# Third weight sum of the odd gate-and-up blocks: from an accumulating transfer to an addition on VectorE

## The chip, the cores and the metric

The kernel runs on one core of one Trainium2 chip. The metric is the device time of one execution in microseconds (us); the median over several runs is compared. Engines are called PE (TensorE), DVE (VectorE), ACT (ScalarE), POOL (GpSimd) and SP (SyncE, which here only issues transfers).

## The reference, cut to what matters

One decoder layer on 512 tokens of width 1024: normalisation, an input projection, two mixers, an output projection, and then the part that the change touches, a dense feed-forward layer:

```
h = h + (silu(xn @ w_gate) * (xn @ w_up)) @ w_down      # xn = rms_norm(h), 512 x 1024
```

w_gate and w_up are 1024 x 2816 float32, w_down is 2816 x 1024. Everything is float32 and is computed as three matmuls over high and low parts.

## The kernel before, in words

**Blocks.** The hidden width of 2816 is cut into 11 blocks of 256 columns, q = 0 to 10. In each block gate and up are made together with a Strassen-like scheme of seven products in place of eight. Its seven weight operands come from four quarters of 512 x 256: gate rows 0 to 511 (b11), gate rows 512 to 1023 (b21), up rows 0 to 511, and up rows 512 to 1023 (b22). The operands are B11 = b11, B21 = b21, T1 = gate(0) + up(0), T2 = T1 + b22, T3 = up(0) + b22, B22 = b22, T4 = T2 + b21.

**Order of the products on PE.** `first_products(q)` runs B11 and B21, `last_products(q)` runs T2, T1, T3, B22, T4. One product is 24 matmuls of 128 x 128 against 256 columns; its result is added up by DVE (L1241 to L1267).

**Operands.** `put` turns each sum into a high part (ACT, L149) and a low part (DVE, L151, a subtraction 128 x 1024). High and low lie together in one of four buffers, two with the name whi and two with the name wlo, taken in turn.

**Loads.** `Weights(q)` loads b11 and b21 (L1145, L1146), `load_rest` loads gate(0) into t1 (L1173), b22 (L1174) and up(0) into t3 (L1175), each 512 KB and all issued by SP. Two accumulating transfers issued by POOL then add up(0) to t1 (L1177) and up(1) to t3 (L1178), in every block but q = 1. The block q = 1 loads up(0) once and makes T1 (L1183) and T3 (L1191) on DVE. `middle` makes t2 = t1 + b22 on DVE (L1184), `end` makes T3, B22 and T4 (L1194 adds b21 to t2).

**Buffers.** In even blocks t1, t2 and t3 are three buffers named t; in odd blocks they are slices of one buffer named L, and one such buffer serves all odd blocks in turn. b11 and b21 share one of three buffers named wraw, and b22 takes another. A load waits until the last reader of the buffer before it is done: L1173 of an odd block for the T4 low part of the odd block before it, L1174 for L1194 of the block before it.

**What sets the order.** The order on each engine is made at build time by a scheduler; instructions marked high priority go ahead as soon as it thinks them ready. The engines then run their own lists strictly in that order. On DVE, the sum L1184 of a block stands well ahead of that block's products: L1184 of an odd block q + 1 stands in front of L1241 and of the B22 low part of the even block q.

The functions that the change touches, and what calls them:

Of the kernel before, what the change touches and what calls it, by code (L numbers as in the profile page):

```python
# [13 lines left out]
OP = mybir.AluOpType  # L14
# [32 lines left out]
def hybrid_layer(ctx: ExitStack, tc: tile.TileContext, x, positions, norm_mix, w_in, mu_shift, w0, w2, a0, a2,  # L47
# [3 lines left out]
    PE, DVE, ACT, POOL = nc.tensor, nc.vector, nc.scalar, nc.gpsimd  # L51
# [16 lines left out]
    def st(shape, tag, bufs=1, dtype=F32):  # L68
        return sb.tile(list(shape), dtype, name=tag, tag=tag, bufs=SB_BUFS.get(tag, bufs))
# [3 lines left out]
    w_in, w_out, w_gate, w_up, w_down = (w.rearrange("l a b -> (l a) b") for w in (w_in, w_out, w_gate, w_up, w_down))  # L73
# [1062 lines left out]
    class Weights:  # L1136
# [25 lines left out]
        def load_rest(self):  # L1162
            self.b22 = st([128, 2048], "wraw")[:, 0:1024].rearrange("p (k n) -> p k n", n=256)
            if self.q % 2:
                tt = st([128, 4, HK, 256], "L")
                self.t1, self.t2, self.t3 = (tt[:, i] for i in range(3))
            else:
                self.t1, self.t2, self.t3 = (st([128, HK, 256], "t4") for _ in range(3))
            if self.q == 1:
                nc.sync.dma_start(self.t3, self.quarter(w_up, 0))  # L1170
                nc.sync.dma_start(self.b22, self.quarter(w_up, 1))
                return
            nc.sync.dma_start(self.t1, self.quarter(w_gate, 0))  # L1173
            nc.sync.dma_start(self.b22, self.quarter(w_up, 1))  # L1174
            nc.sync.dma_start(self.t3, self.quarter(w_up, 0))  # L1175
            with tc.high_priority():
                POOL.dma_start(self.t1, self.quarter(w_up, 0), accum_op=OP.add)  # L1177
                POOL.dma_start(self.t3, self.quarter(w_up, 1), accum_op=OP.add)  # L1178

        def middle(self, tag=None):  # L1180
            with tc.high_priority():
# [5 lines left out]

        def end(self):
            with tc.high_priority():
                if self.q == 1:  # L1190
                    DVE.tensor_add(self.t3, self.t3, self.b22)  # L1191
                self.put("T3", self.t3)
                self.put("B22", self.b22)
                DVE.tensor_add(self.t2, self.t2, self.b21)  # L1194
                self.put("T4", self.t2)
# [135 lines left out]
    for n, (a, b) in enumerate(GROUPS):  # L1331
        one, two = halves[n]
        a11, a21, a12, a22 = (h[:, :, x] for h in (one, two) for x in (left, right))
        lead, end = n == 0, n == 1
        t1, t2 = block4(a, 0, "wraw"), block4(b, 1, ("gin", "kB")[n])
        t3 = st([128, 4, 512], "wraw") if lead else None
        t3 = [t3[:, 2 * i:2 * i + 2] if lead else st([128, 2, 512], "t4") for i in range(2)]
        for i in range(2):
            nc.sync.dma_start(t3[i], down(a, 1)[:, 2 * i:2 * i + 2])
        t2s.append(t2)  # L1340
        DVE.tensor_sub(a21, a22, a21)
        multiply(m1, a_side(a11), b_side(t1), lead, end)
        DVE.tensor_add(a11, a21, a11)
        with tc.high_priority():
            for i in range(2):
                h = slice(2 * i, 2 * i + 2)
                DVE.tensor_add(t1[:, h], t1[:, h], t3[i])
                POOL.dma_start(t3[i], down(b, 1)[:, h], accum_op=OP.add)
            DVE.tensor_add(t2, t2, t1)
        multiply(m5, a_side(a21), b_side(t1), lead, end)  # L1350
        multiply(m6, a_side(a11), b_side(t2), lead, end)
        DVE.tensor_sub(a21, a11, a22)
        multiply(m7, a_side(a21), b_side(t3), lead, end)
# [81 lines left out]
```

## Time and profile before

| | |
|---|---|
| median of 3 runs | 745.86 us (743.71 to 747.25) |
| the profiled execution's own time | 746.93 us |
| its span, first to last instruction | 745.2 us |
| PE busy | 720.3 us, 97% |
| DVE busy | 591.9 us, 79% |
| ACT busy | 402.0 us, 54% |
| POOL busy | 150.8 us, 20% |
| transfers issued by POOL (queue q0) | 12.58 MB, 10.9% of the 16 transfer engines' span |
| transfers issued by SP (queue q1) | 71.91 MB, 29.4% |

The gate-and-up blocks lie between about 415 and 625 us of the span. A busy PE is not a PE at its peak, since its matmuls overlap and their ends are modelled; a product's length is read from the starts of its first matmul and of the next product's. Times in the rows are microseconds from the span's start.

### The profile page before, as it was taken

To read this page: it belongs to the slowest core of one execution; us is meant where nothing else is said; L and a number is where in the kernel's file an instruction comes from. 1 tells how busy PE (TensorE), PEld (TensorE's weight loads), DVE (VectorE), ACT (ScalarE), POOL (GpSimd) and SP (SyncE) were. 2 spreads that over 40 slices of the span, in tenths; PEclk is the share of its full clock that TensorE was granted. 3 is DMA by queue.
4 is the path that set the end of the run, shared out by engine and by line. 5 is a ranking of instruction groups with operands and counts; after the bars stand their busy time and mean duration, and the time that the engine had idled before them with its cause. 6 is when DMAs were issued, how large, how long until landed. Compare 5 with 4: busy or idle time off the path is not lost.

```text
span 745.2 us, 14931 instructions
## 1 busy us (share of the span) xinstructions
PE 720.3 (97%) x6045; PEld 627.3 (84%) x6045; DVE 591.9 (79%) x1097; ACT 402.0 (54%) x670; POOL 150.8 (20%) x250
## 2 busy tenths in 40 slices
PE   6999999998989999999999999989999999999996
PEld 6967887898878788777788999989999999777885
DVE  4488778889767998888368999769796899999835
ACT  6388835325267865778438644444453455465414
POOL 3210030228434552354000001211110101000000
PEclk8999999999899999999999999999999999999998
DMA  7623543100044000140320668787868619352402
GB/s 254 200 88 113 168 115 113 58 2 1 2 144 114 3 2 2 34 138 1 111 88 1 157 188 221 185 181 173 213 166 215 143 63 324 122 118 109 142 0 113
DMA packets 71882, 85.44 MB, mean 115 GB/s; under 512 B 4948, under 2 KB 61350, under 8 KB 71814
## 3 DMA queue, kind: packets, MB, share of 16 engines
q1 hardware_dynamic: 60166, 71.91, 29.4%
q0 software_dynamic: 11648, 12.58, 10.9%
q8 instruction: 47, 0.77, 0.4%
q14 instruction: 21, 0.17, 0.1%
HBM read 82.39 MB, written 2.10 MB: 113 GB/s over the span
## 4 chain that ended last, share of the span: by engine, by line
PE 60%; DVE 22%; DMA 7%; issue 5%; ACT 4%; POOL 1%; SPq 0%; DVEq 0%; POOLq 0%; ACTq 0%
PE ps_ra L169 5%; PE ps_ra L170 5%; PE ps_ra L168 5%; PE ps_pj L170 5%; PE ps_pj L168 5%; PE ps_pj L169 5%; DVE wlo L151 4%; PE ps_o L1019 3%; DVE whi L151 3%; PE ps_pj L1010 2%; DVE L L151 2%; DMA L<-in_w_up_dram 2%; PE ps_s L170 2%; PE ps_s L168 2%; PE ps_s L169 2%
## 5 line engine op out<-in xcount | busy, mean ns | idle before, releaser
L149 ACT ACTIVATE whi<-wraw 128x1024 fp32r<-128x1024 f32 (+1 forms) x63 | 62.6, 1030 | 38.9 <-PE ps_ra L170 13.9
L151 DVE TENSOR_TENSOR wlo<-wraw,whi 128x1024 fp32r<-128x1024 f32 (+1 forms) x46 | 55.2, 1227 | 19.2 <-ACT whi L149 14.3
L1007 POOL TENSOR_SCALAR whi<-whi,m,gates 128x128 f32<-128x128 f32 (+3 forms) x64 | 46.3, 758 | 49.5 <-DVE m L1004 40.1
L170 PE MATMUL ps_ra<-L,wlo 128*128 128x512 f32 (+2 forms) x136 | 47.8, 352 | 0.0
L168 PE MATMUL ps_pj<-L,whi 128*128 128x512 f32 (+1 forms) x128 | 44.3, 351 | 0.5 <-DVE t L1261 0.4
L169 PE MATMUL ps_pj<-L,whi 128*128 128x512 f32 (+1 forms) x128 | 44.7, 349 | 0.0
L169 PE MATMUL ps_ra<-L,whi 128*128 128x512 f32 (+2 forms) x128 | 44.1, 344 | 0.0
L168 PE MATMUL ps_ra<-L,whi 128*128 128x512 f32 (+2 forms) x128 | 43.8, 344 | 0.0
L170 PE MATMUL ps_pj<-L,wlo 128*128 128x512 f32 (+1 forms) x128 | 43.2, 337 | 0.1
L1003 ACT ACTIVATE whi<-whi,m 128x128 f32<-128x128 f32 (+3 forms) x64 | 35.5, 556 | 7.2 <-DVE m L1002 6.8
L168 PE MATMUL ps_ra<-whi,L 128*128 128x256 f32 (+1 forms) x108 | 35.3, 330 | 0.5 <-ACT L L149 0.5
L169 PE MATMUL ps_ra<-wlo,L 128*128 128x256 f32 (+1 forms) x108 | 34.8, 323 | 0.2 <-DVE wlo L151 0.2
L170 PE MATMUL ps_pj<-whi,L 128*128 128x256 f32 (+1 forms) x108 | 34.9, 323 | 0.0
L169 PE MATMUL ps_pj<-wlo,L 128*128 128x256 f32 (+1 forms) x108 | 34.8, 322 | 0.0
L168 PE MATMUL ps_pj<-whi,L 128*128 128x256 f32 (+1 forms) x108 | 34.8, 325 | 0.0
L170 PE MATMUL ps_ra<-whi,L 128*128 128x256 f32 (+1 forms) x108 | 34.5, 322 | 0.0
L1002 DVE CUSTOM_DVE_ANT_0 whi<-ps_s,negb 128x128 f32<-128x128 f32 (+3 forms) x64 | 29.4, 484 | 3.0 <-PE ps_pj L1010 2.0
L170 PEld LDWEIGHTS ps_ra<-L,wlo 128*128 128x128 f32 (+1 forms) x136 | 25.1, 184 | 4.1 <-issue 0.5
L168 PEld LDWEIGHTS ps_pj<-L,whi 128*128 128x128 f32 x128 | 24.0, 188 | 4.3 <-DVE t L1261 0.8
L170 PE MATMUL ps_s<-L,whi 128*128 128x256 f32 (+1 forms) x88 | 26.2, 299 | 1.3 <-DVE whi L151 1.3
L1177 POOL DMA_DIRECT2D t<-in_w_up_dram x6 | 8.0, 1331 | 94.8 <-DVE b L1103 58.5
L170 PEld LDWEIGHTS ps_pj<-L,wlo 128*128 128x128 f32 x128 | 24.0, 188 | 3.5 <-DVE wlo L151 0.9
(708 smaller groups left out, 2546.7 us busy)
## 6 DMA issues: line engine op xcount, KB each, us to landing
wraw<-in_w_gate_dram SPq DMA_DIRECT2D x22, 512.0 KB
wraw<-in_w_in_dram SPq DMA_DIRECT2D x9, 1024.0 KB
wraw<-in_w_down_dram SPq DMA_DIRECT2D x9, 1024.0 KB
t<-in_w_up_dram POOLq DMA_DIRECT2D x12, 512.0 KB, 6.1
wraw<-in_w_up_dram SPq DMA_DIRECT2D x11, 512.0 KB
wraw<-in_w_out_dram SPq DMA_DIRECT2D x4, 1024.0 KB
L<-in_w_up_dram POOLq DMA_DIRECT2D x8, 512.0 KB, 6.8
wraw<-in_w_in_dram SPq DMA_DIRECT2D x6, 512.0 KB
```

The source lines that it names most:

```text
L149: ACT.activation(hi, src, AF.Copy)
L151: (POOL if pool else DVE).tensor_sub(lo, src, hi.bitcast(F32))
L168: PE.matmul(o, lh, rh, start=start, stop=False)
L169: PE.matmul(o, lh, rl, start=False, stop=False)
L170: PE.matmul(o, ll, rh, start=False, stop=stop)
L1002: DVE.tensor_tensor_reduce(pr[:, i], pS[:, i], negb[:, S - n:S], scale=-1.0, scalar=3e38, op0=OP.add, op1=OP.min, accum_out=m[:, i, 0:1])
L1003: ACT.activation(pr[:, i], pr[:, i], AF.Exp, scale=-1.0, bias=m[:, i, 0:1], accum_out=m[:, i, 1:2])
L1007: POOL.tensor_scalar(pr[:, i], pr[:, i], m[:, i, 2:3], gv[:, 1 + b0 + i, h:h + 1], op0=OP.mult, op1=OP.mult)
L1010: PE.transpose(pT[:, j], prr[:, x, j * 128:j * 128 + 128], ident)
L1019: PE.matmul(po[q, 2 * g:2 * g + 2], vtok[:, j % (t + 1), b0 + j // (t + 1), g], pTs[:, par, j], start=False, stop=g == 1 and bs[-1] == 1 a ...
L1177: POOL.dma_start(self.t1, self.quarter(w_up, 0), accum_op=OP.add)
```

## The change

In odd blocks from q = 3 on (3, 5, 7, 9) the accumulating transfer into t3 is left out, and DVE adds b22 to t3 before the operand T3 is made. Both inputs of this addition are loaded by SP as before. Even blocks and q = 1 stay as they are.

```
             with tc.high_priority():
                 POOL.dma_start(self.t1, self.quarter(w_up, 0), accum_op=OP.add)
-                POOL.dma_start(self.t3, self.quarter(w_up, 1), accum_op=OP.add)
+                if self.q % 2 == 0:
+                    POOL.dma_start(self.t3, self.quarter(w_up, 1), accum_op=OP.add)
 ...
         def end(self):
             with tc.high_priority():
-                if self.q == 1:
+                if self.q % 2:
                     DVE.tensor_add(self.t3, self.t3, self.b22)
                 self.put("T3", self.t3)
                 self.put("B22", self.b22)
```

## Rows read from the trace of the kernel before

**Rows 1.** Busy time by stretch: busy us and instructions by engine, granted clock, transfers.

```profile
500.00:516.00 16.00, 15.14 (x118) 15.14 (x119) 14.89 (x18) 8.55 (x10) 1.30 (x1) 0.89 0.83 198
```

**Rows 2.** Timeline of PE, products of B22: start, length, instruction, wait before it.

```profile
498.10 0.28 PE L168 MATMUL ps_pj<-b,wlo 128*128 128x256 f32 x1
...
500.86 0.39 PE L170 MATMUL ps_pj<-b,wlo 128*128 128x256 f32 x1 [2.37 <-DVE wlo L151]
...
501.98 0.42 PE L169 MATMUL ps_pj<-b,wlo 128*128 128x256 f32 x1
...
504.97 0.40 PE L168 MATMUL ps_ra<-L,whi 128*128 128x256 f32 x1
...
540.89 0.28 PE L168 MATMUL ps_s<-b,wlo 128*128 128x256 f32 x1
...
543.72 0.28 PE L168 MATMUL ps_pj<-L,whi 128*128 128x256 f32 x1
...
579.52 0.28 PE L168 MATMUL ps_ra<-b,wlo 128*128 128x256 f32 x1
...
583.49 0.28 PE L168 MATMUL ps_s<-L,whi 128*128 128x256 f32 x1
```

**Rows 3.** Timeline of DVE, the sums into t2 and t3 and one low part.

```profile
427.48 1.21 DVE L1191 TENSOR_TENSOR L<-L,wraw 128x1024 f32<-128x1024 f32 x1
...
475.05 1.23 DVE L1184 TENSOR_TENSOR t<-t,wraw 128x1024 f32<-128x1024 f32 x1 [4.26 <-DMA t<-in_w_up_dram]
...
497.85 1.23 DVE L1184 TENSOR_TENSOR L<-L,wraw 128x1024 f32<-128x1024 f32 x1 [6.97 <-DMA L<-in_w_up_dram]
...
499.59 1.22 DVE L151 TENSOR_TENSOR wlo<-wraw,wlo 128x1024 fp32r<-128x1024 f32 x1
...
536.64 1.23 DVE L1184 TENSOR_TENSOR L<-L,wraw 128x1024 f32<-128x1024 f32 x1 [3.77 <-DMA wraw<-in_w_up_dram]
...
577.77 1.23 DVE L1184 TENSOR_TENSOR L<-L,wraw 128x1024 f32<-128x1024 f32 x1 [5.84 <-DMA L<-in_w_up_dram]
```

**Rows 4.** Timeline of POOL, its accumulating transfers: start of the issue.

```profile
456.24 1.30 POOL L1178 DMA_DIRECT2D L<-in_w_up_dram  x1 [6.67 <-issue]
466.07 1.28 POOL L1177 DMA_DIRECT2D t<-in_w_up_dram  x1 [8.53 <-DVE t L1261]
...
481.62 1.29 POOL L1177 DMA_DIRECT2D t<-in_w_up_dram  x1 [4.99 <-DVE whi L151]
491.98 1.30 POOL L1177 DMA_DIRECT2D L<-in_w_up_dram  x1 [9.08 <-issue]
498.14 1.29 POOL L1178 DMA_DIRECT2D L<-in_w_up_dram  x1 [4.85 <-issue]
```

**Rows 5.** Line L1177 from 470 to 478 us: when its wait ended.

```profile
L1177 POOLq EVENT_SEMAPHORE  x1: 43/43/43, 475.5 to 475.5; - x1
```

**Rows 6.** Line L1177 from 485 to 495 us: when its wait ended.

```profile
L1177 POOLq EVENT_SEMAPHORE  x1: 43/43/43, 486.1 to 486.1; - x1
```

**Rows 7.** Line L1178, whole span: issue to landing.

```profile
DMA to landing us min/median/max: 5.8/5.8/9.5
```

**Rows 8.** Chain that ended last: start, length, what.

```profile
458.75 7.30 issue
...
567.84 9.91 DMA L<-in_w_up_dram
...
590.80 4.39 DMA wraw<-in_w_up_dram
```

**Rows 9.** Timeline of SP's issues: b22 is L1174, t1 is L1173.

```profile
488.07 0.37 SPq L1174 DMA_DIRECT2D wraw<-in_w_up_dram  x1
...
519.49 0.37 SPq L1173 DMA_DIRECT2D L<-in_w_gate_dram  x1
...
529.24 0.37 SPq L1174 DMA_DIRECT2D wraw<-in_w_up_dram  x1
...
558.17 0.37 SPq L1173 DMA_DIRECT2D L<-in_w_gate_dram  x1
```

More of the change, by code (lines that the diff above doesn't have):

```diff
@@ L1177, in load_rest @@
                 POOL.dma_start(self.t1, self.quarter(w_up, 0), accum_op=OP.add)
-                POOL.dma_start(self.t3, self.quarter(w_up, 1), accum_op=OP.add)
+                if self.q % 2 == 0:
+                    POOL.dma_start(self.t3, self.quarter(w_up, 1), accum_op=OP.add)
         def middle(self, tag=None):
@@ L1189, in end @@
             with tc.high_priority():
-                if self.q == 1:
+                if self.q % 2:
                     DVE.tensor_add(self.t3, self.t3, self.b22)
```

## The prediction, made before the changed kernel was run

> **What bounds the kernel now.** I read first the busy time by stretch, then PE's timeline at the starts of products, then who waited for whom on DVE, and last the timelines of POOL and SP and the chain that ended last. PE is the bound of the gate-and-up stage: a product of B22 runs from 540.89 to 543.72, 2.83 us, and two blocks take 38.6 us (540.89 to 579.52) [rows 2]. PE falls behind this in two places only, both inside the B22 product of an even block. In q = 4 that product runs from 498.10 to 504.97, 6.87 us or 4.04 too long: its third matmul, the first to use the low part, comes at 500.86 instead of about 498.3, so 2.5 us are a wait for DVE; the other 1.5 are slow matmuls behind the wait (0.42 in place of 0.28 us), where the granted clock, 0.89 on average over that stretch, lies for a moment at 1.2 GHz in place of 2.4 [rows 1, 2]. In q = 8 it runs from 579.52 to 583.49, 1.14 us too long [rows 2]. More than 5.2 us is not to be had from this stage's stalls.
>
> Both stalls have one pattern. DVE stands at L1184 of the next, odd block, which waits for a transfer; behind it stand L1241 and the B22 low part that PE wants. From the start of L1184 at 497.85 to the end of that low part (499.59 + 1.22) are 2.96 us [rows 3]. So L1184 of q = 5 would have to start by 498.3 - 3.0 = 495.3, and was 2.5 late; L1184 of q = 7 (536.64) had about 1.5 us to spare; that of q = 9 (577.77) was about 1.0 late [rows 2, 3].
>
> **What the late L1184 waits for.** For q = 5 it is the accumulating transfer L1177, issued at 491.98 [rows 3, 4]. Its own precondition, the plain load of t1, was met at 486.1 [rows 6]; for the 5.9 us between, POOL was still busy with L1177 of q = 6, issued at 481.62 [rows 4]. POOL issues its next transfer only when the one before has landed: 491.98 and 498.14 are 6.2 us apart, the first landed at 497.85 at the latest, when it released L1184, and the quickest landing of L1178 takes 5.8 [rows 3, 4, 7]. L1177 of q = 4 shows it best: its precondition was met at 458.75, and it then stood 7.30 us, until 466.07, behind L1178 of q = 3, issued at 456.24 [rows 4, 8]. So the odd L1178 takes a turn in a line that ends at the late L1184.
>
> **What the change removes.** Four accumulating transfers and their turns on POOL. Step by step for the first: L1177 of q = 4 goes at 458.75 and, with its old landing time of 9.0 us (466.07 to 475.05), is done at 467.7. L1178 of q = 4 follows, 5.8 to 9.5 us, done at 473.5 to 477.2 [rows 3, 4, 7, 8]. L1177 of q = 6 has its own precondition at 475.5 and needs up to the 10.4 us between 481.62 and 491.98, so POOL is free for q = 5 at 485.9 to 487.6 in place of 491.98, just when that transfer's own precondition comes (486.1) [rows 4, 5, 6]. It then lands after 5.84 us as before (491.98 to the L1184 it released), or after 9.91 as in q = 9 [rows 3, 4, 8]: at 492 to 497.5. By then b22 is the other condition: issued at 488.07, with 4.4 us (the load at 590.80) to 7.4 us (529.24 to 536.64) it lands at 492.5 to 495.5 [rows 3, 8, 9]. I take 494 for L1184 of q = 5, since the transfer with 5.84 us is the same one as before. That is ahead of 495.3: the stall of q = 4 goes, with its slow matmuls, -4.0 us; bounds 0 and -4.04.
>
> The other three turns buy nothing that I can see: after L1178 of q = 5, 7 and 9 POOL has only L1178 of the next even block to issue, for which nobody waits. And L1177 of q = 9 waits for its own plain load, not for a turn: it goes at 567.84, 9.7 us after L1173 at 558.17 [rows 8, 9].
>
> **What the change adds.** Four additions on DVE, 128 x 1024 from two buffers, priced by the same line in q = 1: 1.21 us [rows 3]. Each waits for t3 and b22 and so stands next to L1184, which also waits for b22; queued behind it are the same L1241 and B22 low part, and PE waits for these. Two places are possible, and no row of before decides between them.
>
> Ahead of L1184: in q = 3 the delay dies in the 4.26 us that DVE waits before L1184 of q = 4 [rows 3]. In q = 5 and 9 the addition runs while DVE waits anyway. In q = 7 it does not: there b22 itself ends the wait [rows 3], so L1184 moves by 1.2 us, inside the 1.5 to spare.
>
> But DVE's progress comes back through the buffer L. From L1184 at 536.64 to the load of t1 of q = 9 at 558.17 are 21.5 us; from a load of t1 to its L1184 are 17.2 us (519.49 to 536.64) or 19.6 (558.17 to 577.77) [rows 3, 9]. This round of 38.7 to 41.1 us is as long as PE's 38.6 or longer, so what is added to it in q = 7 comes out at L1184 of q = 9: +1.2 us on the stall of q = 8. Sum with the additions ahead: -4.0 + 1.2 = -2.8.
>
> Behind L1184: the addition of q = 5 makes the round to q = 7 longer by 1.2, and that of q = 7 delays the low part by 1.2 more; 2.4 less the 1.5 to spare makes a new stall of 0.9 in q = 6. Seen from PE, which moved by 0.9, the load of t1 of q = 9 is then 1.5 late, and the addition of q = 9 adds 1.2: the stall of q = 8 grows by 2.7 to 3.8, longer than the 2.5 behind which the clock fell in q = 4, so perhaps 1.4 us of slow matmuls too. Sum: -4.0 + 0.9 + 2.7 = -0.4, or +1.0 with the clock.
>
> What would cover an addition is DVE's wait; with the cover gone each costs 1.2 us on the round. Fewer bytes count for nothing in this sum: no transfer that ends a wait after 500 us runs beside one that is removed.
>
> I take about the middle of -2.8 and the two ends of the other place: -1.3 us, as neither place is shown. The profiled execution took 746.93 us, 1.07 over the median of the runs; 746.93 - 1.3 = 745.6, and on the median's footing 744.5.
>
> The Trainium skill, "DMA: Bandwidth & Descriptors", section "Issuing engines are not separate DMA queues", says that transfers of all engines run on the same 16 transfer engines and interleave, and that issuing from several engines saves only the issuing time. By that alone a removed L1178 would free bytes and no turn, and the sum would be 0 to +1.2; the rows of L1177 in q = 4 show POOL's own transfers one after the other [rows 4, 8].
>
> **The rivals.** A, the forecast: the stall of q = 4 goes, part of it comes back at q = 8: 743 to 746, chance 0.40.
>
> B, the whole gain stays: the additions lie in waits and the stall of q = 8 does not grow, or goes as well: -4.0 to -5.2, 740.7 to 741.9, chance 0.24. For it: the two waits of 6.97 and 5.84 us [rows 3]. Against it: the round through the buffer L.
>
> C, the turn was not what counted: b22 or a longer landing of L1177 holds L1184 of q = 5 at its old place. The stall of q = 4 stays, and the additions cost 0 to 1.2: 745.9 to 747.1, chance 0.18. For it: upper bounds of 495.5 and 497.5 above. Against it: the 5.9 us that L1177 stood ready. The skill's section named above points this way.
>
> D, slower: C, and the additions behind L1184 in all blocks. The low part of q = 4 comes 1.2 later; at q = 9 two additions on the round and its own, less PE's 1.2, make 2.4, and the stall there of 3.5 brings the clock down for 1.4: +5.0, 750.9, chance 0.12. It decides from the point where L1184 of q = 5 starts after 494.1 (495.3 less one addition) and the addition follows it; up to there C or A holds.
>
> The remaining 0.06 is for a new order made by the scheduler, half to either side.
>
> **How the numbers follow.** About 0.5% (3.7 us) is what a measurement of this kernel can tell from no change: below 742.1 or above 749.6. Faster: B and half the remainder, 0.27. Slower: D and the other half, 0.15. The same: A and C, 0.58. The range reaches from just below B's 740.7 to between C's 747.1 and D's 750.9: 740.5 to 749. It leaves out most of D and of the remainder, under 0.2. A's own range is 743 to 746. The prediction is A's 744.5.
>
> **What would show it.** Right: L1177 of q = 4 goes within 1 us of the landing of its t1; L1177 of q = 5 waits for its own t1; L1184 of q = 5 starts before PE's B22 product of q = 4 less 3 us; that product takes under 4 us and the clock stays at 1.00; four more rows of L1191 at 1.2 us next to L1184; the B22 product of q = 8 takes 4 to 7 us. Wrong: POOL issues a transfer while its last one is still on the way; L1184 of q = 5 released by b22 as late as before; DVE's order of L1184, L1241 and the low part changed altogether, or POOL's order of q = 5 and q = 6, for then the places of all waits have to be read anew.

## The result, and the profile after

The changed kernel took 751.24 us (median of 6 runs, 749.22 to 752.81), the kernel before 746.38 us in the 6 runs beside them. The ratio is 1.0069, with a 95% interval of 1.0047 to 1.0091: slower by 0.7%. The forecast was 744.5 us, with a range of 740.5 to 749: wrong in sign and outside the range. The profiled execution took 749.88 us (span 748.2 us), before 746.93 (745.2).

Lines from L1179 on carry a number higher by one in the changed kernel: the sum into t2 is L1185 in place of L1184, the addition L1192 in place of L1191, the accumulation into t3 L1179 in place of L1178, and L1242 is the old L1241.

PE's timeline of the changed kernel at the four B22 products of even blocks: the product's first matmul, its third if it waited, and the first of the product behind (columns as in [rows 2]).

```profile
459.02 0.28 PE L168 MATMUL ps_ra<-b,wlo 128*128 128x256 f32 x1
...
461.60 0.39 PE L170 MATMUL ps_ra<-b,wlo 128*128 128x256 f32 x1 [2.18 <-DVE wlo L151]
...
464.21 0.28 PE L168 MATMUL ps_s<-L,whi 128*128 128x256 f32 x1
...
500.31 0.28 PE L168 MATMUL ps_pj<-b,wlo 128*128 128x256 f32 x1
...
501.86 0.38 PE L170 MATMUL ps_pj<-b,wlo 128*128 128x256 f32 x1 [1.16 <-DVE wlo L151]
...
504.48 0.28 PE L168 MATMUL ps_ra<-L,whi 128*128 128x256 f32 x1
...
540.57 0.28 PE L168 MATMUL ps_s<-b,wlo 128*128 128x256 f32 x1
...
543.27 0.38 PE L170 MATMUL ps_s<-b,wlo 128*128 128x256 f32 x1 [2.31 <-DVE wlo L151]
...
545.89 0.28 PE L168 MATMUL ps_pj<-L,whi 128*128 128x256 f32 x1
...
581.98 0.28 PE L168 MATMUL ps_ra<-b,wlo 128*128 128x256 f32 x1
...
583.84 0.38 PE L170 MATMUL ps_ra<-b,wlo 128*128 128x256 f32 x1 [1.47 <-DVE wlo L151]
...
586.46 0.28 PE L168 MATMUL ps_s<-L,whi 128*128 128x256 f32 x1
```

Against 2.83 us without a wait, these products are 2.36, 1.34, 2.49 and 1.65 us too long, 7.84 together. Before there were two, 4.04 and 1.14, together 5.18 [rows 2]. The 2.66 us between are nearly all of the 3.0 by which the span grew. The B22 products of q = 2, 4, 6 and 8 now all wait for their low part from DVE. Behind the waits only the first matmul is longer (0.38 to 0.39 us), and the granted clock around each of the four is 1.00; the busy time by stretch shows it for q = 4, where it was 0.89 before [rows 1] (the stretch from 480 is for the explanation below):

```profile
480.00:498.00 18.00, 18.00 (x159) 18.00 (x158) 11.65 (x15) 7.37 (x8) 1.29 (x1) 1.00 0.93 231
...
500.00:516.00 16.00, 14.84 (x128) 14.64 (x127) 14.79 (x19) 7.78 (x9) 0.00 (x0) 1.00 0.60 153
```

DVE's timeline of the changed kernel, sums, additions and low parts of B22:

```profile
458.05 1.22 DVE L1185 TENSOR_TENSOR L<-L,wraw 128x1024 f32<-128x1024 f32 x1 [4.95 <-DMA L<-in_w_up_dram]
459.19 1.22 DVE L1192 TENSOR_TENSOR L<-L,wraw 128x1024 f32<-128x1024 f32 x1
460.32 1.22 DVE L151 TENSOR_TENSOR wlo<-wraw,wlo 128x1024 fp32r<-128x1024 f32 x1
...
497.71 1.23 DVE L1185 TENSOR_TENSOR L<-L,wraw 128x1024 f32<-128x1024 f32 x1 [5.42 <-DMA L<-in_w_up_dram]
498.85 1.22 DVE L1192 TENSOR_TENSOR L<-L,wraw 128x1024 f32<-128x1024 f32 x1
499.99 0.68 DVE L1242 TENSOR_TENSOR t<-ps_s,t 128x512 f32<-128x512 f32 x1
500.59 1.21 DVE L151 TENSOR_TENSOR wlo<-wraw,wlo 128x1024 fp32r<-128x1024 f32 x1
...
539.13 1.23 DVE L1185 TENSOR_TENSOR L<-L,wraw 128x1024 f32<-128x1024 f32 x1 [6.58 <-DMA L<-in_w_up_dram]
...
579.70 1.23 DVE L1185 TENSOR_TENSOR L<-L,wraw 128x1024 f32<-128x1024 f32 x1 [5.30 <-DMA L<-in_w_up_dram]
```

Three things answer to [rows 3]. L1185 of q = 5 starts at 497.71, hardly earlier than the 497.85 of before, where 494 was forecast. The addition stands directly behind it, in front of L1242 and the low part, and delays them by 1.14 us from start to start; this is so in all four odd blocks. And in q = 3 the sum and the addition now stand in front of the B22 low part of q = 2, which ran ahead of both before: the stall at 459.02 is new.

POOL's timeline of the changed kernel, for [rows 4]:

```profile
459.47 1.30 POOL L1177 DMA_DIRECT2D t<-in_w_up_dram  x1 [9.66 <-DVE L L1185]
465.89 1.28 POOL L1179 DMA_DIRECT2D t<-in_w_up_dram  x1 [5.12 <-DVE wlo L151]
477.96 1.29 POOL L1177 DMA_DIRECT2D t<-in_w_up_dram  x1 [10.79 <-DMA t<-in_w_gate_dram]
490.57 1.29 POOL L1177 DMA_DIRECT2D L<-in_w_up_dram  x1 [11.32 <-DVE b L1268]
```

The turn was freed as foreseen: L1177 of q = 4 goes at 459.47 in place of 466.07, that of q = 6 at 477.96 in place of 481.62. But that of q = 5 goes at 490.57, only 1.4 earlier. Its own wait and its landing, from the view of L1177's instructions between 485 and 495, stand against [rows 6] and the 5.84 us of before:

```profile
L1177 POOLq EVENT_SEMAPHORE  x1: 43/43/43, 489.9 to 489.9; - x1
...
DMA to landing us min/median/max: 7.1/7.1/7.1
```

The plain load of t1 was met at 489.9 in place of 486.1, and the accumulation on top of it took 7.1 us. SP's issues of these loads (the odd blocks' t1; compare [rows 9]):

```profile
480.11 0.37 SPq L1173 DMA_DIRECT2D L<-in_w_gate_dram  x1
...
520.57 0.37 SPq L1173 DMA_DIRECT2D L<-in_w_gate_dram  x1
...
561.91 0.37 SPq L1173 DMA_DIRECT2D L<-in_w_gate_dram  x1
```

With these rows the round through the buffer L can be laid out. Its DVE part, from the sum into t2 to the next odd block's load of t1, was 21.5 us for q = 7 before, and is now 22.78 (539.13 to 561.91); for q = 5 it is 22.86 (497.71 to 520.57), where it was 21.64 (497.85 to 519.49), and for q = 3 it is 22.06 (458.05 to 480.11). DVE works through it with hardly a gap (14.79 of the 16 us from 500 to 516), so that little in it can hide an addition. Its transfer part, from that load to the sum, is 17.6, 18.56 and 17.79 us, in the range of the 17.2 to 19.6 of before. A round is thus 39.7 to 41.4 us against PE's 38.6.

### The profile page after: what moved, and what is told of

The parts are those of the page before. It is cut to its first block, busy times and chain, and to the rows that moved or that the text cites. A ratio compares the mean times of both kernels' runs of the same rounds, so it can differ in the third digit from the quotient of the medians.

```text
span 748.2 us, 14927 instructions
## 1 busy us (share of the span) xinstructions
PE 721.0 (96%) x6045; PEld 628.0 (84%) x6045; DVE 595.7 (80%) x1101; ACT 402.0 (54%) x670; POOL 146.9 (20%) x246
## 4 chain that ended last, share of the span: by engine, by line
PE 60%; DVE 24%; DMA 8%; issue 3%; ACT 3%; POOL 0%; SPq 0%; DVEq 0%; ACTq 0%; POOLq 0%
PE ps_ra L170 5%; PE ps_ra L169 5%; PE ps_ra L168 5%; PE ps_pj L170 5%; PE ps_pj L168 5%; PE ps_pj L169 5%; DMA L<-in_w_up_dram 5%; DVE wlo L151 4%; PE ps_o L1019 3%; PE ps_pj L1010 2%; DVE whi L151 2%; DVE L L151 2%; PE ps_s L170 2%; PE ps_s L168 2%; PE ps_s L169 2%
## 5 line engine op out<-in xcount | busy, mean ns | idle before, releaser
L1177 POOL DMA_DIRECT2D t<-in_w_up_dram x6 | 8.0, 1335 | 116.0 <-DVE b L1103 58.7
```

## The experiments

In the expectations three theories go by short names. **Place** (theory 1): what costs is that the addition stands ahead of the B22 low part on DVE. **Load or round** (theory 2): what costs is that it makes DVE's part of the round through the buffer L longer, wherever it stands in it. **Removal** (theory 3): the missing transfers themselves change the order or the landings for the worse. Of the edits, `last["B22"]` is the low-part instruction of the block's B22, and `issue_after(x)` places an instruction behind x in its engine's list.

Too long in the table is, in the profiled execution, the sum over the products of q = 2 to 9 that exceed 2.83 us by over 0.4. Ratios are to runs of the kernel before on the same chip, whose medians were 746.54 to 746.84 us beside the experiments.

| kernel | median, us | ratio to before (95%) | too long, us | profiled execution, us |
|---|---|---|---|---|
| before | 746.38 | | 5.2 | 746.93 |
| changed | 751.24 | 1.0069 (1.0047 to 1.0091) | 7.8 | 749.88 |
| e1_removal_only | 746.21 | 0.9987 (0.9970 to 1.0005) | 4.0 | 745.11 |
| e2_add_only | 770.83 | 1.0321 (1.0291 to 1.0351) | 27.5 | 768.97 |
| e3_add_behind_b22 | 750.29 | 1.0040 (1.0015 to 1.0064) | 6.8 | 749.76 |
| e4_add_on_pool | 748.16 | 1.0024 (1.0001 to 1.0046) | 4.6 | 748.85 |
| e5_before_order | 742.97 | 0.9953 (0.9931 to 0.9974) | 0 | 743.46 |
| e6_after_order | 744.57 | 0.9960 (0.9943 to 0.9978) | 0 | 743.43 |
| e7_removal_order | 741.76 | 0.9934 (0.9911 to 0.9957) | 0 | 740.11 |
| e8_after_q3_order | 749.99 | 1.0058 (1.0035 to 1.0082) | 6.2 | 750.29 |
| e9_after_slices | 741.19 | 0.9938 (0.9917 to 0.9958) | 0 | 741.24 |
| e10_before_slices | 740.25 | 0.9920 (0.9896 to 0.9944) | 0 | 740.25 |
| e11_after_slices_order | 740.75 | 0.9926 (0.9902 to 0.9949) | 0 | 740.32 |
| e12_after_two_adds | 754.70 | 1.0094 (1.0059 to 1.0129) | 12.3 | 754.50 |

The last column less the one before it lies between 740.1 and 744.3 us in all fourteen, while the times themselves spread over 29 us: these few products carry most of what the kernels differ in. Small waits included, the stretch from the start of the B22 product of q = 2 to that of q = 10 takes 154.5 us in the kernels without stalls (155.0 in e6), 160.1 before and 163.5 in the changed kernel.

### The two halves of the change

**e1_removal_only**: the accumulation is gone and no addition takes its place.

```
-                if self.q % 2:
+                if self.q == 1:
                     DVE.tensor_add(self.t3, self.t3, self.b22)
```

> The four accumulating transfers into t3 are left out and the four additions too, so T3 of blocks 3, 5, 7, 9 lacks b22. DVE's list is that of before but for one place: L1184 of q = 3 stands ahead of the B22 low part of q = 2, as in the changed kernel. Theory 1 (place: what costs is DVE work put between L1184 of an odd block and the B22 low part of the even block before it): a new stall of about 2.3 us in q = 2, the stall of q = 4 smaller than 4.0 as POOL's turn is free, nothing new in q = 6, so 744 to 747 us. Theory 2 (load: every addition makes DVE's round through the buffer L longer, wherever it stands): 742 to 745. Theory 3 (the removal itself costs, by the new place of L1184 of q = 3 or by the other timing of the transfers): 749 to 751, as the changed kernel.

It measured 0.9987 (0.9970 to 1.0005): the removal, which the prediction booked at -4.0 us, buys nothing that can be told from zero, and costs nothing either; as a cause of the loss it is out. POOL's, DVE's and PE's timelines around the product that was to lose its stall, one fence each:

```profile
488.86 1.29 POOL L1177 DMA_DIRECT2D L<-in_w_up_dram  x1 [11.28 <-DVE wlo L151]
```

```profile
497.01 1.23 DVE L1185 TENSOR_TENSOR L<-L,wraw 128x1024 f32<-128x1024 f32 x1 [6.80 <-DMA L<-in_w_up_dram]
```

```profile
497.28 0.28 PE L168 MATMUL ps_pj<-b,wlo 128*128 128x256 f32 x1
...
500.02 0.58 PE L170 MATMUL ps_pj<-b,wlo 128*128 128x256 f32 x1 [2.34 <-DVE wlo L151]
500.40 0.41 PE L168 MATMUL ps_pj<-b,wlo 128*128 128x256 f32 x1
...
504.12 0.28 PE L168 MATMUL ps_ra<-L,whi 128*128 128x256 f32 x1
```

The accumulation for q = 5 goes 3.1 us earlier than the 491.98 of before and lands 8.1 us later (488.86 to 497.01) where it took 5.84. The sum into t2 gains 0.8 us, and PE is earlier by as much (e1 enters the stage 0.9 us ahead of the kernel before), so the stall stays with its slow matmuls (0.41 us). The stall of q = 8, 1.14 us before, is gone. The stall of 2.3 us expected in q = 2 did not come, though the sum of q = 3 stands ahead of the low part there (455.35 and 456.50, PE's product from 458.65): the sum comes 3.3 us before the product, in the changed kernel 1.0.

**e2_add_only**: the kernel before with `if self.q % 2:` around the addition; both accumulations stay.

> The kernel before, with the four additions of b22 to t3 added and all accumulating transfers kept, so T3 of blocks 3, 5, 7, 9 has b22 twice. L1184 of q = 3 stays behind the B22 low part of q = 2; the additions of q = 5, 7, 9 stand right behind L1184. Theory 1: stalls of q = 4, 6, 8 longer by 1.2 us each and by what the round adds, +3 to +5: 749 to 751. Theory 2: the same, 749 to 751. Theory 3: no change, 746 to 747.

All expectations missed by some 20 us, and the run doesn't price the addition: with the accumulation kept, the addition also waits for that transfer, which POOL issues only behind L1177. DVE's timeline around q = 5:

```profile
504.37 1.23 DVE L1184 TENSOR_TENSOR L<-L,wraw 128x1024 f32<-128x1024 f32 x1 [3.92 <-DMA L<-in_w_up_dram]
...
510.51 1.23 DVE L1191 TENSOR_TENSOR L<-L,wraw 128x1024 f32<-128x1024 f32 x1 [4.91 <-DMA L<-in_w_up_dram]
```

DVE stands for 4.91 us more (2.55 to 6.50 in the four blocks). It does show how dear a wait in this place is: 19.2 us of second waits and about 4.9 us of additions make 24 us, and the median lies 24.2 over the 746.65 of the kernel before on the same chip. That the two agree so closely is partly chance, since slow matmuls behind three of the waits are in the time too.

**e12_after_two_adds**: the changed kernel with the addition done twice.

```
-                    DVE.tensor_add(self.t3, self.t3, self.b22)
+                    for _ in range(1 if self.q == 1 else 2):
+                        DVE.tensor_add(self.t3, self.t3, self.b22)
```

> The changed kernel with the addition done twice in q = 3, 5, 7 and 9 (T3 has b22 twice there). Round theory: every second addition is 1.1 us more on each of the rounds from q = 3 to q = 9 and at the end, +4.5, 754 to 757, and the time from L1184 of q = 5 to the load of t1 of q = 7 grows from 22.9 to 24.0. Place theory: the same size, from four longer stalls. If DVE had room for it: 751.

The second addition did not go in front of the low part, as DVE's timeline around q = 5 shows; behind it SP's issue of the next t1:

```profile
500.70 1.23 DVE L1185 TENSOR_TENSOR L<-L,wraw 128x1024 f32<-128x1024 f32 x1 [7.15 <-DMA L<-in_w_up_dram]
501.84 1.22 DVE L1193 TENSOR_TENSOR L<-L,wraw 128x1024 f32<-128x1024 f32 x1
502.98 0.69 DVE L1243 TENSOR_TENSOR t<-ps_s,t 128x512 f32<-128x512 f32 x1
503.58 1.22 DVE L151 TENSOR_TENSOR wlo<-wraw,wlo 128x1024 fp32r<-128x1024 f32 x1
504.71 1.22 DVE L1193 TENSOR_TENSOR L<-L,wraw 128x1024 f32<-128x1024 f32 x1
```

```profile
524.93 0.43 SPq L1173 DMA_DIRECT2D L<-in_w_gate_dram  x1
```

So it could cost only through the round. It did: the DVE part grew again, by 1.37 us in each of the rounds behind q = 5 and q = 7 (500.70 to the load at 524.93 is 24.23; 24.16 for the next), and the median rose by 3.5 us over the changed kernel. The intervals of the two ratios overlap, and about 1.5 us of the profiled rise are slow matmuls behind the stall of q = 8, so it is the longer round that the run shows, and not its price. This speaks for the round and against the place as the whole cause.

### Where the addition stands

**e3_add_behind_b22**: the changed kernel with the addition alone put behind the B22 low part.

```
+                    with tc.issue_after(last["B22"]) if self.q > 1 else nullcontext():
                         DVE.tensor_add(self.t3, self.t3, self.b22)
```

> The changed kernel with the addition queued behind the B22 low part of the even block before it, everything else the same; L1184 of q = 3 stays ahead of the B22 low part of q = 2. Theory 1: the stalls of q = 2, 4, 6, 8 each lose the 1.1 us of the addition, -3.5 to -4.5 against the changed kernel: 746.5 to 748. Theory 2: the round is as long as in the changed kernel, 750 to 751.5. Theory 3: 750 to 751.5.

At 1.0040 its interval overlaps that of the change. DVE's timeline of e3_add_behind_b22, the sums of q = 5 and q = 9:

```profile
497.57 1.23 DVE L1185 TENSOR_TENSOR L<-L,wraw 128x1024 f32<-128x1024 f32 x1 [5.67 <-DMA L<-in_w_up_dram]
...
579.89 1.22 DVE L1185 TENSOR_TENSOR L<-L,wraw 128x1024 f32<-128x1024 f32 x1 [5.43 <-DMA L<-in_w_up_dram]
```

They are 82.32 us apart (497.57 to 579.89), in the changed kernel 81.99, in the kernel before 79.92: the two rounds are as long with the addition behind the low part as in front of it. Single stalls moved: 0.85 in q = 2 and 0.46 in q = 4, but 4.24 in q = 6, slow matmuls included. What the profiled execution of e3 saves lies at the two ends of the chain of rounds: from the B22 product of q = 2 to that of q = 4 it takes 40.20 us in place of 41.29, and from q = 8 to q = 10 39.52 in place of 40.57, each time about one addition. So the place counts at the ends, some 2 us in all, and the round in between.

**e8_after_q3_order**: in q = 3 alone, the sum and the addition go behind the B22 low part of q = 2, as the kernel before had them.

```
+                with tc.issue_after(last["B22"]) if self.q == 3 else nullcontext():
                     DVE.tensor_add(self.t2, self.t1, self.b22)
...
+                    with tc.issue_after(last["B22"]) if self.q == 3 else nullcontext():
                         DVE.tensor_add(self.t3, self.t3, self.b22)
```

> The changed kernel with one move: the B22 low part of q = 2 stands ahead of L1184 and the addition of q = 3 again, as in the kernel before; the additions of q = 5, 7, 9 stay right behind L1184. Place theory: the stall of 2.4 us in q = 2 goes, and half or less of it comes back at q = 4: 748.5 to 750. Round theory: the start of the round at L1184 of q = 3 is not earlier by this, so 750 to 751.5.

At 1.0058 it stays where the change is. The stall of q = 2 falls to about 0.6 us, those of q = 4, 6 and 8 are 1.6 to 2.1. The new order in q = 3, with the addition in it, is where the first stall comes from (e1 has the order without the addition, and no stall there), and not what the change costs.

**e6_after_order**: the same for the sum into t2 and the addition of all odd blocks from q = 3 on (`if self.q % 2 and self.q > 1` and `if self.q > 1`).

> The changed kernel with L1184 of the odd blocks and the addition both queued behind the B22 low part of the even block before. Theory 1: no wait of PE for a B22 low part is left, in q = 2, 4, 6 or 8; what is late next is the T4 low part, by at most 1 us: 741 to 744. Theory 2: the waits come back at T4 as long as they were at B22: 748 to 751. Theory 3: as theory 2.

0.9960 (0.9943 to 0.9978), faster than both kernels. DVE's timeline of e6_after_order:

```profile
492.48 1.23 DVE L151 TENSOR_TENSOR wlo<-wraw,wlo 128x1024 fp32r<-128x1024 f32 x1 [0.45 <-ACT wlo L149]
...
496.23 1.23 DVE L1186 TENSOR_TENSOR L<-L,wraw 128x1024 f32<-128x1024 f32 x1 [2.53 <-DMA L<-in_w_up_dram]
```

The low part is done before DVE stands at the sum, and all that PE waits between 440 and 612 us is one line of its list of waits:

```profile
PE ps_s L170 <- DVE whi L151: 0.2, 1, 0.2
```

**e5_before_order** and **e7_removal_order** put the sum into t2 there in the kernel before and in e1_removal_only.

> The kernel before, with L1184 of the odd blocks queued behind the B22 low part of the even block before it; all accumulating transfers kept, no addition added. Place theory (what counts is DVE work and its waits between L1184 of an odd block and the B22 low part): the two stalls of before, 4.0 and 1.1 us, go, and the time falls by 3.5 to 5: 741.5 to 743. Round theory (DVE and the transfers through the buffer L set the pace): the waits come back at the T4 low part, 745 to 746.5.

> No accumulating transfer into t3 and no addition in blocks 3, 5, 7, 9 (so T3 lacks b22 there), and L1184 of the odd blocks behind the B22 low part. Differs from the ordered form of the changed kernel (744.6) by the four additions alone. Place theory: an addition that stands behind the B22 low part costs nothing, so 743.5 to 745. Round theory: each addition is 1.1 us on the round, 741 to 742.5 here. Beside the ordered form of the kernel before, it shows what the removed transfers alone are worth once the order is out of the way: nothing, or up to 2 us.

They measured 0.9953 and 0.9934, without a stall in these products. The stall of before thus needs this order, the sum that waits for a transfer in front of work that doesn't; the slices below remove it with the order left as it is. The order also shortens DVE's part of the round, behind q = 5 and q = 7 to 20.0 to 20.1 us in e5 and e7 and 21.1 to 21.3 in e6, since the low part is then made ahead of the sum; so these three runs don't tell place from round. Against e5, e7 shows what the removal is worth once nothing waits there, and e6 against e7 what the addition costs: 1.2 and 2.8 us, in both cases with intervals that overlap. Of the 3.3 us between the profiled executions of e6 and e7, 1.8 lie ahead of the stage (its first product starts at 403.95 and 402.18) and 1.0 behind it, so the 2.8 can't be read as the price of the addition.

**e4_add_on_pool**: the additions of q = 3, 5, 7 and 9 go to POOL, out of DVE's list.

```
-                    DVE.tensor_add(self.t3, self.t3, self.b22)
+                    (POOL if self.q > 1 else DVE).tensor_add(self.t3, self.t3, self.b22)
```

> The changed kernel with the additions of q = 3, 5, 7, 9 on POOL in place of DVE; DVE's list is then that of the kernel with neither transfers nor additions (746.2). Place theory: DVE has nothing more in front of the B22 low part, 745.5 to 747.5, unless POOL's addition holds up its next accumulating transfer. Round theory: the same, since the round has no addition on DVE. If POOL's addition slows DVE's additions or transfers: 748 or more.

At 1.0024 (1.0001 to 1.0046) two thirds of the loss are gone, and DVE's part of the round is 21.7 us again. POOL's timeline around q = 5:

```profile
495.86 2.39 POOL L1192 TENSOR_TENSOR L<-L,wraw 128x1024 f32<-128x1024 f32 x1 [1.10 <-DMA wraw<-in_w_up_dram]
```

It takes 2.39 us there. Products are 4.6 us too long, which is less than before, yet the kernel is 1.6 us slower. Of the 1.9 us between the profiled executions 1.0 lies in the stage: with the waits too small for the table it takes 161.1 us from B22 of q = 2 to that of q = 10, before 160.1. The last two pairs of blocks have no stall of over 0.4 us and still take 39.27 and 39.15 us against PE's 38.6; the loads of t1 are 39.23 and 39.27 apart, so PE follows the round. Another 0.7 us lies ahead of the stage.

### The round itself

**e9_after_slices**: the changed kernel, additions at their place, but with one buffer L for all odd blocks whose slices are followed one by one, t2 alternating between two slices. A load of t1 then waits only for the readers of t1.

```
-                tt = st([128, 4, HK, 256], "L")
-                self.t1, self.t2, self.t3 = (tt[:, i] for i in range(3))
+                if self.q == 1:
+                    last["tt"] = st([128, 4, HK, 256], "L")
+                self.t1, self.t2, self.t3 = (last["tt"][:, i] for i in (0, self.q // 2 % 2 * 2 + 1, 2))
```

> The changed kernel, but the odd blocks share one buffer L whose slices are tracked one by one, with t2 in two slices by turns: the load of t1 of an odd block then waits for the readers of its own slice and no longer for the T4 low part of the odd block before. The additions stay right behind L1184; L1184 of q = 3 comes behind the B22 low part of q = 2 again, as in the run that moved only that (750.0). Round theory (the round through the buffer L, 40.5 to 41 us against PE's 38.6, sets the pace): the waits at L1184 of q = 5, 7, 9 fall under 3 us, the pace falls to PE's, and the time to 742 to 745. Place theory (the additions in front of the B22 low part cost by themselves): 748 to 750.5.

741.19 us, 0.9938 (0.9917 to 0.9958): 10 us less than the changed kernel. DVE's timeline around q = 5, and SP's issue of the next t1 (L1186 and L1193 are the sum and the addition, L1174 the load):

```profile
494.15 1.23 DVE L1186 TENSOR_TENSOR L<-L,wraw 128x1024 f32<-128x1024 f32 x1 [1.54 <-DMA wraw<-in_w_up_dram]
495.29 1.22 DVE L1193 TENSOR_TENSOR L<-L,wraw 128x1024 f32<-128x1024 f32 x1
...
497.03 1.22 DVE L151 TENSOR_TENSOR wlo<-wraw,wlo 128x1024 fp32r<-128x1024 f32 x1
```

```profile
509.40 0.37 SPq L1174 DMA_DIRECT2D L<-in_w_gate_dram  x1
```

The load goes 15.25 us behind the sum in place of 22.86, the sum is released by b22 and not by the accumulation, and the addition stands where it stood and costs nothing. One reserve: with the buffers the scheduler's order changed too (in q = 3 the sum is again behind the low part of q = 2, and SP and POOL issue the odd loads earlier). e8_after_q3_order has the first of these alone, and its median is only 1.2 us below the change's. A second one: the stretch from B22 of q = 2 to that of q = 10 falls from 163.5 to 154.5 us, but 2.8 us of the gain lie behind it (122.9 us to the end of the span in place of 125.7), outside the rounds.

**e10_before_slices** is the same edit in the kernel before, **e11_after_slices_order** joins it with the order of e6_after_order.

> The kernel before with the same slices, all accumulating transfers kept and no addition. Round theory: the stalls of q = 4 and 8 go, 741.5 to 743.5. Place theory: the wait for L1177 behind POOL's other transfers still holds L1184, 745 to 746.5.

> The changed kernel with the slices and with L1184 of the odd blocks and the addition behind the B22 low part. Round theory: both undo the same waits, so about the faster of the two alone, 742 to 744.5, with four additions of DVE time still in the list. If the additions cost by DVE's load alone, slower than the sliced kernel without additions by up to 4.6 us; by the round theory equal to it within 1.5.

At 740.25 and 740.75 us they can't be told from e9_after_slices. The kernel before with slices is the fastest of all, 0.9920 (0.9896 to 0.9944). With the round cut, accumulation or addition is all one: the difference of 4.9 us falls to 0.9, inside the intervals, and the stretch from B22 of q = 2 to that of q = 10 takes 154.5 us in both. In e10 the sum of q = 5, 7 and 9 still stands ahead of the low part, so the stalls of before go without a change of that order.

## Why the prediction was wrong

**What bounds the stage** was right: all stalls of the stage, before and in the changed kernel, are in B22 products of even blocks, for a low part that stands behind the odd block's sum on DVE. e5, e6 and e7 take that order away, and the stalls with it.

**The step that failed: "the stall of q = 4 goes, with its slow matmuls, -4.0 us".** POOL's turns came free nearly as worked out (for q = 6 at 477.96 in place of 475.5). But the step kept two old times in its sum: that the plain load of t1 for q = 5 would be there at 486.1, and that the accumulation would take 5.84 us. They came out at 489.9 and 7.1, in e1 at 488.2 and 8.1, so the sum that PE's low part stands behind was as late as before (497.71 for 497.85). The stall of q = 4 reads 1.34 us in the changed kernel, for 4.04, only because PE comes to it after the new stall of 2.36 in q = 2 and its matmuls stay fast; in e1, without either, it is 4.01. The stretch of 480 to 498 us in the kernel before (the last columns are the granted clock, the transfer engines' busy share and GB/s):

```profile
480.00:498.00 18.00, 18.00 (x160) 18.00 (x159) 10.99 (x14) 5.64 (x7) 2.59 (x2) 1.00 0.96 240
```

The transfer engines are as good as full, with 0.96, and in the changed kernel they are with 0.93. A POOL transfer that goes earlier there (L1177 of q = 6, from 481.62 to 477.96) meets plain loads that ran alone before. The bytes of the two queues from 482 to 486 us show it (packets, MB, the time that the packets took as a share of the 16 transfer engines' time; q1 has SP's plain loads, q0 POOL's accumulations), first in the kernel before, where q0 has none:

```profile
q1 hardware_dynamic: 1310, 1.31, 102.5%
```

and in the changed kernel:

```profile
q0 software_dynamic: 486, 0.49, 76.4%
q1 hardware_dynamic: 451, 0.45, 40.0%
```

The plain loads move a third of what they moved, and the load of t1, issued 0.3 us later, is there 3.8 us later; in e1 the two share the engines in the same way from 479 to 483 (0.41 and 0.46 MB). The whole way, from the load to the sum L1184 or L1185, was 18.07 us before, 17.6 after, 17.91 in e1. So the turn was given back as bytes. The prediction's rule that POOL issues a transfer only when the one before has landed held for L1177 and L1178 in these blocks, but not for all of POOL's transfers: before, L1348 is issued at 619.28 and again at 620.87, and lands after 5.6 us at the earliest. The Trainium skill, "DMA: Bandwidth & Descriptors", section "Issuing engines are not separate DMA queues", says that transfers of all engines share the same 16; the prediction weighed it and held the rows of the turn against it. e1, at 0.9987, agrees with it in effect.

**The price of an addition** was right (1.21 us forecast, 1.22 measured), and so was the way it costs: DVE's part of the round is 1.2 us longer. What was wrong is the choice of "about the middle" between the two places. All four additions stand behind the sum, for which the prediction's own sum was -0.4 to +1.0 even with the gain, and +5.0 without it.

**"In q = 3 the delay dies in the 4.26 us"** was right for the wait, which is gone at L1185 of q = 4, but the scheduler also moved the sum and the addition of q = 3 ahead of the B22 low part of q = 2: 2.36 us of new stall in the first round. That was in the 0.06 kept for a new order.

**Rival D**, 750.9 at a chance of 0.12, gave the size: 751.24. Its parts, no gain and the additions behind the sum, are what happened. Their spread was not foreseen: D had the stall of q = 4 longer by 1.2, none in q = 2, and a fall of the clock in q = 8; the trace has four stalls of 1.3 to 2.5 us and a clock of 1.00. That the sums agree so well is partly chance.

**What stays open.** The profiled executions differ by 3.0 us and the medians by 4.9: the profiled one of the changed kernel lies 1.4 under its median, that of before 0.5 over, and no view shows the rest. The scatter between the profiled executions without stalls (740.1 to 743.5 us) lies outside the products that the change touches: the first product of the stage starts between 402.18 us (e7) and 405.66 (e5), with a granted clock of 0.97 and 0.95 from 100 to 200 us, and from B22 of q = 10 to the end of the span are 122.9 (e9) to 126.3 us (e6). Why these parts differ, in code that the edits leave alone, stays open. So does how the loss divides between the round and the ends of the chain, beyond the 2 us that e3 shows in a single execution.

## What to carry to other kernels

When a buffer serves every second block, lay out its round (load, transfer, wait, the engine's list up to the last reader, the next load) and hold it against the period of the engine that bounds the stage: work added anywhere in a round that is already longer made the round longer by its own time here (1.2 to 1.4 us for an addition of 1.2), and cost nothing that shows once the round was cut. A turn in a queue is worth only what the transfers behind it can use: here the transfer engines were already full, and with the earlier issue the last transfer landed as late as before. And an instruction that waits for a transfer, placed ahead of work that doesn't, is the first thing to move: in the kernel before the order alone was worth 3.6 us (746.54 to 742.97), the finer buffers 6.6 (746.84 to 740.25, about 2.5 of it behind the stage).

## What was not expected of the hardware

The same accumulating transfer of 512 KB for q = 5 took 5.84 us before, 7.1 in the changed kernel and 8.1 with the removal alone. An accumulated byte held the transfer engines about twice as long as a loaded one: 0.49 MB took 76.4% of their time in the lines above, 1.31 MB of plain loads 102.5%. The same addition of 128 x 1024 took 2.39 us on POOL and 1.22 on DVE.

The length of a wait alone did not tell whether TensorE's clock would fall. Behind the waits of 2.34 us in e1, 2.37 before, 2.51 in e3 and 3.60 in e12 (q = 8) most of the product's matmuls ran at 0.41 to 0.42 us, the lower of TensorE's two levels. Behind those of 2.18 and 2.31 in the changed kernel, 2.49 in e4 and even 3.03 in e12 (q = 4) they stayed at 0.28. So the prediction's "longer than the 2.5 behind which the clock fell" was no safe sign.
